# Attention on one core: value products of four key blocks in one run, row maxima of two score products by one VectorE instruction

## The chip, the cores and the metric

One core of one Trainium2 chip runs the whole program. The metric is the device time of one execution in microseconds (us); a run's time is that of this core. Smaller is better.

## The reference, cut to what matters

One decoder layer over 4096 tokens of width 1024: an RMSNorm, one input projection, three token mixers that share its columns, one output projection with a residual, and a final RMSNorm. The change touches only the third mixer, a causal attention with a cumulative forget bias, eight heads of width 64:

```python
for blk in range(seq // 128):
    s = einsum('bhqd,bhkd->bhqk', qh[blk], kh[:, :, :q1]) * scale
    s = s + c[:, :, q0:q1, None] - c[:, :, None, :q1]     # c: cumulative log forget gate
    s = where(mask, s, -inf)                              # causal inside the last block
    p = softmax(s, axis=-1)
    outs.append(einsum('bhqk,bhkd->bhqd', p, vh[:, :, :q1]))
```

Everything is float32.

## The kernel before, in words

Phase 1 (the first 1660 us of the profiled span) projects the tokens, runs the other two mixers and stores the attention's operands in DRAM. Phase 3 (the last 360 us) is the output projection. Phase 2 between them is the attention, and the change is there.

Phase 2 walks through 32 *units*: a pair of heads p (4 of them) by a group Q of 512 queries (8 of them), in the order p, then Q. A unit (p, Q) has 4(Q+1) *steps*, one for each block kb of 128 keys, 576 steps in all. The last four steps of a unit are its diagonal ones, where the number of live queries falls from 512 to 384, 256 and 128. Four steps that share one tile of 512 keys are called a *group* here; there are 144.

Two computations run side by side in the steps:

- The **second pass** (the loop `for si, (u, kb)`, whose products stand on lines 1353 and 1356). For each of two heads TensorE makes a score tile `st` [128 keys, 512 queries] in PSUM from two accumulating products (`ka` with `qa`, `kb` with `qc`). ScalarE writes `pt = exp(st + bias)` to SBUF (L1360). In diagonal steps GpSimd sets the masked corner of `pt` to zero (L1365). One step later `do_pv` adds two 64-column value products into the PSUM tile `pv` (L1238; the heads use the two halves of the array's columns; the operands are plain float32 where all score products are float32r) and adds `pt` into running sums `acc`, head 0 on VectorE and head 1 on GpSimd (both L1247).
- The **row-maximum pass** (the generator `rowmax`) works on later units. Each of its steps is one product `sm` [128 queries, 512 keys] (L128) into a PSUM bank, and one VectorE maximum along its rows into a column of `mp` (L137; where the last key tile is diagonal, a masked maximum, L132). The main loop advances it twice in each step, once before and once after `do_pv`, and a third time while it is less than LEAD = 76 products ahead. At the end of a unit `rm_tail` combines the maxima (`mm`, `m2`) and, some products later, transposes them on TensorE (`mt`, L1166); VectorE copies them out (`mr`, L1168).

When a unit's last value product is issued, `finish_unit` starts, one stage in each later step: two products of `ones_v` with the sums (`pl`, L1206), then on ScalarE a logarithm and an exponential of it (L1210, L1211), on VectorE `rt<-pl` (L1213) and L1214, on GpSimd two products (L1215, L1216), on VectorE `rt<-pv` (L1218), and the store.

PSUM has eight banks: two buffers of `st`, two of `pv`, and four one-bank buffers of the pool `ps_sm`, which `sm`, `mt`, `pl` and phase 3's `o` take in turn. `pt` has seven buffers. TensorE's order is as the program writes it (`manual_schedule`); the order of the other engines' instructions is chosen by the tile framework's scheduler, and each engine then executes its list in order.

## Time and profile before

| | |
|---|---|
| three runs | 3496.33, 3509.1 and 3524.09 us (median 3509.1) |
| span of the profiled execution (no separate time of it is listed) | 3516.6 us |
| mean granted TensorE clock | 0.982 |
| phase 2, 1660 to 3158 us: TensorE busy | 1469.9 of 1498 us |
| the same stretch: VectorE / ScalarE / GpSimd busy | 1251.7 / 737.3 / 897.9 us |

How to read it: TensorE has two rows, PE for the products and PEld for the loading of weights, which goes on beside the products. Matmul rows carry a modelled end, so the cost of a product is read from the start of one to the start of the next rather than from its own duration. A row "x4" of `pv` is the two heads' products of one key block: each is executed as two, and the two heads' run at the same time.

### The profile page before, as it was taken

The page shows a single profiled execution, that of the slowest core. Times are in us where ns is not written, and L with a number is a line of the kernel's source. Part 1 is how long each engine was busy: PE and PEld are TensorE (multiplying, and loading weights), DVE is VectorE, ACT ScalarE, POOL GpSimd, SP SyncE. Part 2 cuts the span into 40 slices and gives each one's busy share as a digit, 9 for nine tenths or more (in the row PEclk, how much of TensorE's full clock was granted, in tenths as well). Part 3 has the DMA queues.
Part 4 walks back from the last instruction along what each step waited for, and adds up shares of the span by engine and source line. Part 5 has one row for each costly group of instructions (what it writes and reads, how often), then busy time and mean ns, then how long its engine had stood idle before and what let it go on. Part 6 is the DMA issues. An engine that isn't in the chain of part 4 may idle for free.

```text
span 3516.6 us, 63564 instructions
## 1 busy us (share of the span) xinstructions
PE 3417.2 (97%) x24375; PEld 2569.8 (73%) x24375; DVE 2482.6 (71%) x5111; ACT 1584.4 (45%) x2883; POOL 1422.0 (40%) x1468
## 2 busy tenths in 40 slices
PE   7999999999999999988999999999999999999999
PEld 7999999999999998988444444444444444448887
DVE  6467746685467756782798878888889888965554
ACT  6335544356435543452345445454544554562221
POOL 2134422333134322352465466555665666570000
PEclk9999999999999999999799899999999999999999
DMA  5332333214332223212731141014101321013442
GB/s 178 109 94 64 97 127 116 79 53 159 97 104 68 70 85 111 67 49 78 155 77 34 49 118 43 19 41 120 55 28 28 97 64 37 28 64 135 148 146 96
DMA packets 227603, 297.75 MB, mean 85 GB/s; under 512 B 19602, under 2 KB 172448, under 8 KB 227298
## 3 DMA queue, kind: packets, MB, share of 16 engines
q1 hardware_dynamic: 227298, 293.69, 27.7%
q8 instruction: 191, 3.13, 0.4%
q14 instruction: 114, 0.93, 0.1%
HBM read 208.96 MB, written 84.43 MB: 83 GB/s over the span
## 4 chain that ended last, share of the span: by engine, by line
PE 76%; DVE 13%; ACT 4%; POOL 3%; issue 2%; DMA 2%; SPq 0%; DVEq 0%; POOLq 0%; ACTq 0%
PE acc L885 15%; PE pv L1238 13%; PE acc L906 12%; PE o L1430 10%; PE sm L128 9%; PE st L1353 7%; PE st L1356 6%; DVE wlo L211 2%; DVE acc L1247 1%; DMA x<-in_x_dram 1%; DVE mp L137 1%; PE pl L1206 1%; DVE gt L729 1%; DVE xq L494 1%; PE plb L557 1%
## 5 line engine op out<-in xcount | busy, mean ns | idle before, releaser
L1360 ACT ACTIVATE pt<-st,bias 128x512 f32<-128x512 f32 (+3 forms) x1152 | 692.0, 648 | 711.3 <-PE st L1356 699.3
L1247 POOL TENSOR_TENSOR acc<-acc,pt 128x512 f32<-128x512 f32 (+3 forms) x544 | 700.4, 1288 | 479.9 <-ACT pt L1360 469.4
L137 DVE TENSOR_REDUCE mp<-sm 128x1 f32<-128x512 f32 x896 | 590.1, 682 | 100.1 <-PE sm L128 92.3
L1238 PE MATMUL pv<-pt,v 128*64 128x512 f32 (+3 forms) x2304 | 587.7, 589 | 7.2 <-POOL pt L1365 4.5
L885 PE MATMUL acc<-hhi,whi 128*128 128x256 f32 x2048 | 580.7, 288 | 4.2 <-DVE q L718 2.3
L885 PE MATMUL acc<-hhi,wlo 128*128 128x256 f32 x2048 | 568.1, 282 | 0.0
L885 PE MATMUL acc<-hlo,whi 128*128 128x256 f32 x2048 | 567.3, 281 | 0.0
L906 PE MATMUL acc<-whi,hhi 128*128 128x256 f32 (+1 forms) x1792 | 518.3, 289 | 18.6 <-DVE gu L727 16.0
L1247 DVE TENSOR_TENSOR acc<-acc,pt 128x512 f32<-128x512 f32 (+3 forms) x544 | 506.5, 931 | 40.9 <-ACT pt L1360 30.4
L128 PEld LDWEIGHTS sm<-kb,qb 66*128 66x128 f32 x1152 | 218.1, 192 | 416.6 <-DVE mp L137 177.4
L906 PE MATMUL acc<-wlo,hhi 128*128 128x256 f32 (+1 forms) x1792 | 507.3, 283 | 0.0
L906 PE MATMUL acc<-whi,hlo 128*128 128x256 f32 (+1 forms) x1792 | 506.9, 283 | 0.0
L128 PE MATMUL sm<-kb,qb 66*128 66x512 f32 (+2 forms) x1152 | 494.2, 436 | 5.9 <-DVE mp L137 4.5
L1353 PE MATMUL st<-qa,ka 128*128 128x512 f32 (+2 forms) x1152 | 449.3, 392 | 12.4 <-DMA ka<-d_kl 12.4
L1356 PE MATMUL st<-qc,kb 68*128 68x512 f32 (+2 forms) x1152 | 442.3, 386 | 1.1 <-DMA qc<-d_m 1.1
L885 PEld LDWEIGHTS acc<-hhi,whi 128*128 128x128 f32 x2048 | 385.0, 190 | 7.8 <-DVE q L718 2.7
L885 PEld LDWEIGHTS acc<-hlo,whi 128*128 128x128 f32 x2048 | 384.2, 190 | 0.3 <-DVE hlo L273 0.2
L885 PEld LDWEIGHTS acc<-hhi,wlo 128*128 128x128 f32 x2048 | 384.3, 190 | 0.0
L906 PEld LDWEIGHTS acc<-whi,hhi 128*128 128x128 f32 x1792 | 341.9, 191 | 22.4 <-DVE gu L727 16.6
L906 PEld LDWEIGHTS acc<-wlo,hhi 128*128 128x128 f32 x1792 | 342.3, 191 | 0.1
L906 PEld LDWEIGHTS acc<-whi,hlo 128*128 128x128 f32 x1792 | 341.7, 191 | 0.0
L211 DVE SCALAR_TENSOR_TENSOR wlo<-wraw,gT,whi 128x256 fp32r<-128x256 f32 (+1 forms) x480 | 268.6, 600 | 58.1 <-ACT whi L210 56.8
(262 smaller groups left out, 4911.1 us busy)
## 6 DMA issues: line engine op xcount, KB each, us to landing
wraw<-in_w_in_dram SPq DMA_DIRECT2D x120, 512.0 KB
x<-in_x_dram SPq DMA_DIRECT2D x88, 512.0 KB
qa<-d_qh SPq DMA_DIRECT2D x64, 256.0 KB
out_dram<-x SPq DMA_DIRECT2D x31, 512.0 KB
kb<-d_kh SPq DMA_DIRECT2D x38, 256.0 KB
d_kh<-chi SPq DMA_DIRECT2D x32, 256.0 KB
d_kl<-clo SPq DMA_DIRECT2D x32, 256.0 KB
d_qh<-chi SPq DMA_DIRECT2D x32, 256.0 KB
```

Source lines behind the costliest of these rows:

```text
L128: nc.tensor.matmul(ps[:, :n], qb[0:66, h, i * P : (i + 1) * P], kb[0:66, h, :n], start=True, stop=True)
L137: nc.vector.tensor_reduce(dst, ps[:, :use], axis=AX.X, op=ALU.max)
L211: nc.vector.scalar_tensor_tensor(lo[:, k, :n], raw, g, hi[:, k, :n].bitcast(F32), op0=ALU.mult, op1=ALU.subtract)
L494: nc.vector.tensor_tensor(xq[rows, :, r, :].rearrange("p g (n h) -> p g n h", h=h), sl(e), sl(qf), op=ALU.mult,)
L885: nc.tensor.matmul(ps[:, a, :], ww[:, k, cs], hh[:, k, :], start=n == 0, stop=n == 3 * KC - 1)
L906: nc.tensor.matmul(o, hh[:, k, ts_], ww[:, k, :width], start=n == 0, stop=n == 3 * KC - 1)
L1238: nc.tensor.matmul(pv[64 * h : 64 * h + 64, q0:], vt[:, kb % 4, 64 * h : 64 * h + 64], pts[h][:, q0:], start=kb == 0, stop=kb == nkb - 1,)
L1247: eng.tensor_tensor(a[:, q0:], a[:, q0:], pts[h][:, q0:], op=ALU.add)
L1353: nc.tensor.matmul(st[:, qm:], ka_t[g][:, h, cs], qa_t[u % 2][:, h, qm:], start=True, stop=False)
L1356: nc.tensor.matmul(st[:, qm:], kb_t[g][0:68, h, cs], qc_t[u % 2][:, h, qm:], start=False, stop=True)
L1360: nc.scalar.activation(pt[:, q0:], st[:, q0:], AF.Exp, bias=bias_of[u][:, h, kb : kb + 1])
L1430: nc.tensor.matmul(ps, a[:, k % 4, o : o + P], b[k][:, cs], start=n == 0, stop=n == 3 * KC - 1)
```

## The change

It has four parts.

1. **Value products by groups.** `do_pv(u, j, group)` is called once for four steps, in the first step of the next group, after that step's scores and row-maximum products. It issues the eight value products of the group one after another. `pt` gets 13 buffers instead of 7.
2. **Sums.** VectorE's four additions of a group are written behind those products, in the same call. GpSimd's addition is written right behind the exponentials of its own step.
3. **Row maxima in pairs.** `rm_pair` makes two `sm` products into the two banks of one tile and takes their maxima by one `tensor_reduce` of 2 x 512 elements (diagonal tiles still get one masked maximum each). A step of the loop advances the pass once, by a pair, and a second time while it is less than LEAD products ahead. The tail's transpose waits three pairs instead of six products.
4. **PSUM.** `ps_sm` has two buffers of two banks instead of four of one; `pl`, `mt` and `o` take turns with the pairs in these two.

```diff
-        ps_sm = p2.enter_context(tc.tile_pool(name="ps_sm", bufs=4, space=PSUM))
+        ps_sm = p2.enter_context(tc.tile_pool(name="ps_sm", bufs=2, space=PSUM))
-        pp = p2.enter_context(tc.tile_pool(name="pp", bufs=7))
+        pp = p2.enter_context(tc.tile_pool(name="pp", bufs=13))
...
+    def rm_pair(ps, qb, kb, hi_, diag, tri, mp, cj):
+        for n in range(2):
+            rm_matmul(ps[:, n, :], qb, kb, hi_ + n, diag)
+        if diag:
+            for n in range(2):
+                rm_max(ps[:, n, :], hi_ + n, True, tri, mp[:, hi_ + n, cj : cj + 1])
+        else:
+            rm_max(ps, hi_, False, tri, mp[:, hi_ : hi_ + 2, cj])
...
-                    for hi_ in range(8):
-                        ps = ps_sm.tile([P, 512], F32, tag="sm", name="sm")
-                        rm_product(
-                            ps, qb, kb_t[p * NJ + cj], hi_, cj == Q, tri, mp[:, hi_, cj : cj + 1]
-                        )
+                    for hi_ in range(0, 8, 2):
+                        ps = ps_sm.tile([P, 2, 512], F32, tag="sm", name="sm")
+                        rm_pair(ps, qb, kb_t[p * NJ + cj], hi_, cj == Q, tri, mp, cj)
...
+        def do_pv(u, j, group):
...
+            for kb, pts in group:
+                q0, _ = q0_of(u, kb)
+                for h in (1, 0):
+                    nc.tensor.matmul(
+                        pv[64 * h : 64 * h + 64, q0:], vt[:, kb % 4, 64 * h : 64 * h + 64], pts[h][:, q0:],
+                        start=kb == 0, stop=kb == nkb - 1,
+                    )
+            for kb, pts in group:
+                do_acc(u, kb, 0, pts[0])
...
+            group.append((kb, pts))
             rm_step()
-            if pend is not None:
-                do_pv(*pend)
-            pend = (u, kb, pts)
-            rm_step()
+            do_acc(u, kb, 1, pts[1])
             if rm_count[0] < 2 * si + LEAD:
                 rm_step()
+            if kb % 4 == 0 and pend is not None:
+                do_pv(*pend)
+                pend = None
+            if kb % 4 == 3:
+                pend, group = (u, kb // 4, group), []
             tick(fin)
```

Other lines move the release of key and value slots into `do_pv`, and drop comments. Phase 1 and phase 3 are the same but for the pool that phase 3's `o` comes from.

TensorE in the middle of a unit, before: `st` are the scores of a step, `sm` row-maximum products, `pv` the value products of the step ahead.

```order
L1238 MATMUL pv<-pt,v 64x512 x2
L128 MATMUL sm<-kb,qb_21728 128x512
L1353 MATMUL st<-qa_21724,ka 128x512
L1356 MATMUL st<-qc_21729,kb 128x512
L1353 MATMUL st<-qa_21724,ka 128x512
L1356 MATMUL st<-qc_21729,kb 128x512
L128 MATMUL sm<-kb,qb_21728 128x512
L1238 MATMUL pv<-pt,v 64x512 x2
L128 MATMUL sm<-kb,qb_21728 128x512
```

The same place with the change:

```order
L1377 MATMUL st<-qc_21730,kb 128x512
L127 MATMUL sm<-kb,qb_21726 128x512 x2
L1374 MATMUL st<-qa_21725,ka 128x512
L1377 MATMUL st<-qc_21730,kb 128x512
L1374 MATMUL st<-qa_21725,ka 128x512
L1377 MATMUL st<-qc_21730,kb 128x512
L127 MATMUL sm<-kb,qb_21726 128x512 x2
L1265 MATMUL pv<-pt,v 64x512 x8
L1374 MATMUL st<-qa_21725,ka 128x512
L1377 MATMUL st<-qc_21730,kb 128x512
L1374 MATMUL st<-qa_21725,ka 128x512
L1377 MATMUL st<-qc_21730,kb 128x512
```

Value products stood alone between row-maximum products in every step; now eight follow each other, and then four steps have none.

TensorE where one unit ends and the next begins, with the change:

```order
L1181 MATMUL mt<-ident,m_31034 16x128
L127 MATMUL sm<-kb,qb_21727 128x512 x2
L1265 MATMUL pv<-pt,v 64x512 x2
L1265 MATMUL pv<-pt,v 64x384 x2
L1265 MATMUL pv<-pt,v 64x256 x2
L1265 MATMUL pv<-pt,v 64x128 x2
L1374 MATMUL st<-qa_21725,ka 128x512
L1377 MATMUL st<-qc_21730,kb 128x512
L1374 MATMUL st<-qa_21725,ka 128x512
L1377 MATMUL st<-qc_21730,kb 128x512
L127 MATMUL sm<-kb,qb_21727 128x512 x2
L1221 MATMUL pl<-acc_30998,ones_v 64x512
```

`mt` and `pl` each take one of the two `ps_sm` buffers between two pairs; `pl` comes in the second step of the new unit.

VectorE at such a boundary, before (`rt<-pl` is the step of `finish_unit` that frees the buffer of `pl`):

```order
L1247 TENSOR_TENSOR acc_29118<-acc_29118,pt 128x512
L137 TENSOR_REDUCE mp<-sm 128x1 x2
L1247 TENSOR_TENSOR acc_29118<-acc_29118,pt 128x512
L137 TENSOR_REDUCE mp<-sm 128x1
L1213 TENSOR_TENSOR rt<-pl,rc 128x512
L137 TENSOR_REDUCE mp<-sm 128x1
L1214 TENSOR_SCALAR rt<-rt 128x512
L137 TENSOR_REDUCE mp<-sm 128x1
```

and with the change:

```order
L1252 TENSOR_TENSOR acc_28510<-acc_28510,pt 128x512
L140 TENSOR_REDUCE mp<-sm 128x2
L1252 TENSOR_TENSOR acc_28510<-acc_28510,pt 128x512
L140 TENSOR_REDUCE mp<-sm 128x2
L1228 TENSOR_TENSOR rt<-pl,rc 128x512
L140 TENSOR_REDUCE mp<-sm 128x2
L1229 TENSOR_SCALAR rt<-rt 128x512
L140 TENSOR_REDUCE mp<-sm 128x2
L1252 TENSOR_TENSOR acc_28510<-acc_28510,pt 128x512
L1233 TENSOR_TENSOR rt<-pv,rc 128x512
L1252 TENSOR_TENSOR acc_28510<-acc_28510,pt 128x512 x2
L140 TENSOR_REDUCE mp<-sm 128x2 x3
```

One maximum stands where two stood. The sums, written together behind the value products, do not stay together: the scheduler puts the sums of the first steps ahead of those steps' maxima and the others between later ones.

## The prediction

> **What bounds the kernel now.** I read the page's busy times first, then the busy times by stretch of time, then the timeline of single steps.

> ```profile
> PE 3417.2 (97%) x24375; PEld 2569.8 (73%) x24375; DVE 2482.6 (71%) x5111; ACT 1584.4 (45%) x2883; POOL 1422.0 (40%) x1468
> ```
> ```profile
> 1660.00:3158.00 1498.00, 1469.85 (x5880) 717.08 (x5879) 1251.73 (x2163) 737.33 (x1226) 897.85 (x930) 0.98 0.24 63
> 2200.00:2500.00 300.00, 297.64 (x1219) 146.47 (x1216) 255.49 (x464) 147.92 (x250) 183.16 (x194) 1.00 0.23 62
> ```

> The columns of the second fence are the stretch, its length, then TensorE's products, its weight loads, VectorE, ScalarE and GpSimd. In attention TensorE is busy 1470 of 1498 us, VectorE 84%, ScalarE 49%. Over 2200 to 2500 us TensorE pauses for 2.4 us in 300: no wait is left to remove, only TensorE's own time. How that is spent shows in one step:

> ```profile
> 2202.30 0.20 PEld L1238 LDWEIGHTS pv<-pt,v 128*64 128x64 f32 x4 [0.36 <-issue]
> 2202.30 1.08 PE L1238 MATMUL pv<-pt,v 128*64 128x512 f32 x4
> 2203.31 0.50 PE L128 MATMUL sm<-kb,qb 66*128 66x512 f32 x1
> 2203.65 0.40 PE L1353 MATMUL st<-qa,ka 128*128 128x512 f32 x1
> 2203.89 0.40 PE L1356 MATMUL st<-qc,kb 68*128 68x512 f32 x1
> 2204.13 0.40 PE L1353 MATMUL st<-qa,ka 128*128 128x512 f32 x1
> 2204.33 1.27 ACT L1360 ACTIVATE pt<-st,bias 128x512 f32<-128x512 f32 x2 [1.35 <-PE st L1356]
> 2204.36 0.39 PE L1356 MATMUL st<-qc,kb 68*128 68x512 f32 x1
> 2204.59 0.39 PE L128 MATMUL sm<-kb,qb 66*128 66x512 f32 x1
> 2204.91 1.08 PE L1238 MATMUL pv<-pt,v 128*64 128x512 f32 x4
> ```

> Read starts. Score and row-maximum products follow each other every 0.235 us. The one after the value products holds its place for 0.34 (3.31 to 3.65), the one ahead of them for 0.32 (4.59 to 4.91), the value products of a block for 1.01. A step is 2.61 us.

> **Part 1, value products in runs.** What does a second block cost right behind the first? Near the end one `pv` is followed by products of the same shape, `pl`:

> ```profile
> 3089.21 1.08 PE L1238 MATMUL pv<-pt,v 128*64 128x512 f32 x4
> 3090.12 1.03 PE L1206 MATMUL pl<-acc,ones_v 128*64 128x512 f32 x4
> 3091.08 0.50 PE L1353 MATMUL st<-qa,ka 128*128 128x512 f32 x1
> ```

> Both take 1.87 us (3089.21 to 3091.08), so the second costs 1.87 - 1.01 = 0.86. Alone, a block costs 1.01 + 0.34 + 0.32 = 1.67 with its two neighbours; in a run 0.86 + 2 x 0.235 = 1.33. Each block that gets a neighbour ahead of it saves 0.34 us: three in each of 144 groups, 432 x 0.34 = **147 us**. A run of four costs 3.59, and with the longer products around it 3.78.

> Does the next block's weight load hide there?

> ```profile
> L1238 PEld LDWEIGHTS pv<-pt,v 128*64 128x64 f32 x2304 | 115.0, 136 | 202.3 <-issue 176.9 <-POOL pt L1365 10.4 <-POOL acc L1247 10.4
> ```

> A load takes 0.136 us; the four of a block are done 0.20 us after 2202.30, under products that run to 2203.38, and the 0.86 above leaves no room for one in the open. [...]

> **What shows behind the bound: ScalarE and two score buffers.** TensorE alone would need 24 x 0.235 + 3.78 = 9.42 us for four full steps, against 4 x 2.61 = 10.45. But four steps now come without value products between them, 6 x 0.235 = 1.41 us each, and a score buffer is not back that fast. A place near the end where a score product waits for its buffer:

> ```profile
> 3133.46 1.26 ACT L1360 ACTIVATE pt<-st,bias 128x512 f32<-128x512 f32 x2
> 3134.19 0.19 PEld L1353 LDWEIGHTS st<-qa,ka 128*128 128x128 f32 x1 [0.86 <-ACT pt L1360]
> 3134.53 0.40 PE L1356 MATMUL st<-qc,kb 68*128 68x512 f32 x1
> 3134.77 0.19 PEld L1353 LDWEIGHTS st<-qa,ka 128*128 128x128 f32 x1 [0.28 <-ACT pt L1360]
> 3134.97 1.32 ACT L1360 ACTIVATE pt<-st,bias 128x512 f32<-128x512 f32 x2 [0.25 <-PE st L1356]
> ```

> The exponentials end at 3134.72, the load starts 0.05 later, the second product 0.34 after the first load (4.19 to 4.53), the exponential 0.44 after that (4.97), and one takes 0.68: 0.05 + 0.34 + 0.44 + 0.68 = 1.51 us round a buffer. The load that waits cannot hide, which is 0.11 of it. From the end of a run (t = 0): scores at 0 and 0.47; exponentials 0.67 to 1.35 and, 0.59 behind, 1.26 to 1.94; the next scores at 1.51 and 2.10, then 3.03 and 3.61, then 4.54 and 5.13; the run at 6.06 instead of 5.64. So 0.42 lost, and a stretch of four full steps takes 9.84. There are 84 stretches with nothing else in them: **+35**. Bounds: 0.12 each if the load hides (+10), 0.42 (+35); I take the row's.

> **Parts 2 and 3, VectorE.** The new maximum over 2 x 512 is in no row. From below, by the slope of the masked maxima; from above, twice the old one:

> ```profile
> L137 DVE TENSOR_REDUCE mp<-sm 128x1 f32<-128x512 f32 x896 | 590.1, 682 | 100.1 <-PE sm L128 92.3
> L132 DVE CUSTOM_DVE_ANT_0 sm<-sm,tri 128x512 f32<-128x512 f32 x64 | 44.5, 695 | 4.0 <-PE sm L128 3.7
> L132 DVE CUSTOM_DVE_ANT_0 sm<-sm,tri 128x256 f32<-128x256 f32 x64 | 27.6, 431 | 6.9 <-PE sm L128 6.9
> L1247 DVE TENSOR_TENSOR acc<-acc,pt 128x512 f32<-128x512 f32 x448 | 457.0, 1020 | 33.7 <-ACT pt L1360 30.4 <-POOL pt L1365 1.8
> L1247 POOL TENSOR_TENSOR acc<-acc,pt 128x512 f32<-128x512 f32 x448 | 623.4, 1392 | 474.4 <-ACT pt L1360 469.4
> L1365 POOL TENSOR_SCALAR_AFFINE_SELECT pt<-pt 128x128 f32<-128x128 f32 x256 | 83.9, 335 | 69.1 <-ACT pt L1360 66.2
> ```

> (695 - 431) / 256 = 1.03 ns an element, so 682 + 528 = 1210 ns; twice 682 is 1364. I take 1.21, since no second start is paid. Instructions in a row start some 0.09 before the last one ends, so 1.13 a maximum. A sum takes 0.69 undisturbed, 0.60 to the next start:

> ```profile
> 2202.43 0.69 DVE L1247 TENSOR_TENSOR acc<-acc,pt 128x512 f32<-128x512 f32 x1
> 2203.04 1.50 DVE L137 TENSOR_REDUCE mp<-sm 128x1 f32<-128x512 f32 x2
> ```

> Four of each: 4 x (1.13 + 0.60) = 6.9 us of 9.84. VectorE was not the bound and is not now, so its saving is worth nothing by itself: the work that hides it is TensorE's 9.42. In a full stretch the fourth pair (4.1) wants the buffer of the second-last maximum (done 3.2): no wait. Were the maximum 1.36, still none.

> **Part 4, two buffers: the boundaries.** `pl` holds one of two buffers until `rt<-pl`. Before, with four:

> ```profile
> 2230.05 1.08 PE L1206 MATMUL pl<-acc,ones_v 128*64 128x512 f32 x4
> 2231.18 0.60 ACT L1210 ACTIVATE rc<-pl 128x512 f32<-128x512 f32 x1 [1.89 <-PE pl L1206]
> 2231.84 1.27 ACT L1360 ACTIVATE pt<-st,bias 128x512 f32<-128x512 f32 x2
> 2232.99 0.63 ACT L1211 ACTIVATE rc<-rc 128x512 f32<-128x512 f32 x1
> 2234.60 0.68 DVE L1213 TENSOR_TENSOR rt<-pl,rc 128x512 f32<-128x512 f32 x1
> ```

> It was held 5.2 us (2230.05 to 2235.28). Now, in a unit's first full stretch, `pl` stands at 1.50 and takes 1.20 of TensorE. The logarithm comes 1.13 later (2.63), scores of the next step at 2.61, exponentials 3.28 to 4.55, ScalarE's second instruction to 5.08. VectorE's order puts a sum (to 4.6) and a maximum (to 5.73) ahead of `rt<-pl`, which ends at 6.42. The pair of the step after wants that buffer at 5.17 and starts 6.42 + 0.05 + 0.11 = 6.58: 1.41 lost, about 1.6 with ScalarE's share. 28 units: **+46**. Queued behind the waiting pair are the next scores, the run and all that feeds on them. Bounds: 0.9 if the sum comes behind `rt<-pl`, 3 if both additions meet GpSimd's.

> In diagonal steps the scores are shorter:

> ```profile
> 2219.49 0.18 PE st L1353
> 2221.87 0.12 PE st L1353
> ```

> Steps are then 1.18, 0.95 and 0.95 us on TensorE, less than a maximum (1.13) behind a sum that waits for GpSimd's 0.34. The third pair waits 0.3 for its buffer and scores wait 0.5 for ScalarE: 0.8 x 32 = **+26**. `mt` uses up a buffer's turn (29 times, always ahead of a run), so the pair behind it needs the maximum just started: about 0.6 each, **+17**. Three units of one group get `pl` in a diagonal stretch: 1.5 each, **+5**. Last, when the row maxima have run out:

> ```profile
> 3109.45 1.08 PE L1238 MATMUL pv<-pt,v 128*64 128x512 f32 x4
> 3111.60 0.65 PE L1238 MATMUL pv<-pt,v 128*64 128x512 f32 x2
> ```

> 2.15 a step, 8.6 a group. With the run, two score buffers at 1.51 give 5.59 + 3.78 = 9.37: each of 8 groups loses 0.77 instead of saving 1.02 - 0.42 = 0.60, together **+11**.

> The opening (three products a step before, two pairs now, until 76 ahead) I leave at 0, between -10 and +10.

> Sum: -147 + 35 + 46 + 26 + 17 + 5 + 11 = **-7 us**, 3509.6 against the span of 3516.6. That execution lies 7.5 us over the median of the runs, so on the runs' scale 3509.1 - 7 = **3502**. About 1%, 35 us, is what a measurement of this kernel tells from no change. Nearly all that the runs save goes back to waits that two score buffers and two `ps_sm` buffers open.

> **Rivals.**

> - *The waits are mostly hidden.* Late loads cost 0.12 instead of 0.42 in a stretch (-25), boundaries half (-23 and -13). 3502 - 61 = 3441. For: VectorE has 3 us of slack in a stretch. Against: the 1.51 us round trip is read off rows. 0.28.
> - *Slower: `pl` keeps its buffer longer.* The additions' rows say 1020 and 1392 ns on average where an undisturbed VectorE one takes 0.69: VectorE and GpSimd disturb each other, and in the new order sums and `rt<-pl` fall where GpSimd adds. If a boundary costs 2 us more than forecast, 31 x 2 = 62: 3564. It decides from (35 + 7) / 31 = 1.4 us more. Against: in the run VectorE catches up. 0.16. [...]
> - *Loads show in the run.* If each further block's load stood in the open, 3 x 0.136 x 144 = 59 us would come on top: 3561. The `pl` rows and the four loads done in 0.20 us speak against it: 0.04. [...]
> - *The change does not do what it says* in one point already: the order shows the sums scattered, not together. Were they executed in the run, boundaries would lose the 0.6 of the sum ahead of `rt<-pl`, 28 x 0.6 = 17 us less; that is inside the forecast's range. Something else that gains over 1%, the opening for one: 0.02.

> **How the numbers follow.** Forecast 0.50, rivals 0.28, 0.16, 0.04 and 0.02. Within 1% is the forecast, 0.50; faster 0.28 + 0.02 = 0.30; slower 0.16 + 0.04 = 0.20. The range holds 8 in 10: down to the first rival's 3441, up to 3550, short of the slower ones' 3561 and 3564. The forecast's own range is 3475 to 3540.

> **What would show it.** Right: the second to fourth blocks of a run 0.86 apart; score loads waiting for `pt` in the steps between runs, with about 9.8 us from run to run; the pair after `pl` waiting over 1 us for `rt`; the new maximum near 1.2 us; TensorE's busy share in attention down from 98% to about 90%. Wrong: a run to run of 9.4, no wait behind `pl`, or blocks in a run 1.0 apart.

## The result, and the profile after

The kernel before took 3512.2 us (median of 6 runs), the changed one 3541.4 (6 runs): ratio 1.0085, 95% interval 1.0065 to 1.0106. That is 29 us slower, clear of the noise, where 7 us faster was forecast. The profiled executions have spans of 3516.6 and 3539.7 us.

The page's busy times of the changed kernel:

```profile
PE 3390.0 (96%) x24375; PEld 2603.3 (74%) x24375; DVE 2377.4 (67%) x4675; ACT 1606.0 (45%) x2883; POOL 1399.5 (40%) x1468
```

TensorE is busy 27 us less and VectorE 105. By stretches of time, with the columns as in the prediction and the granted clock behind GpSimd's count:

```profile
1660.00:3182.00 1522.00, 1444.37 (x5895) 751.81 (x5893) 1146.48 (x1727) 759.32 (x1226) 875.32 (x930) 0.97 0.23 62
2066.50:3177.00 1110.50, 1065.08 (x4354) 548.23 (x4352) 841.45 (x1256) 571.57 (x922) 657.45 (x693) 0.98 0.18 53
```

The second row is the part of attention that belongs to the last three pairs of heads (p = 1 to 3). The same units in the kernel before:

```profile
2073.00:3153.10 1080.10, 1071.44 (x4353) 519.67 (x4352) 912.33 (x1567) 555.01 (x922) 673.80 (x690) 1.00 0.19 54
```

They take 1110.5 instead of 1080.1 us, 30.4 more, and the clock over them is no longer full: the records of the granted clock list nine windows of 3.4 or 6.8 us at half clock there, 54.6 us together, and none before. The first pair of heads is 8.5 us shorter (390.8 against 399.3), the rest of the span 1.2 longer: 30.4 - 8.5 + 1.2 = 23.1.

**The runs and the score buffers are as forecast.** A full stretch, from a run to the next:

```profile
2247.25 3.65 PE L1265 MATMUL pv<-pt,v 128*64 128x512 f32 x16
2250.83 0.50 PE L1374 MATMUL st<-qa,ka 128*128 128x512 f32 x1
2252.34 0.19 PEld L1374 LDWEIGHTS st<-qa,ka 128*128 128x128 f32 x1 [0.28 <-ACT pt L1381]
2252.34 0.50 PE L1374 MATMUL st<-qa,ka 128*128 128x512 f32 x1
2253.85 0.50 PE L1374 MATMUL st<-qa,ka 128*128 128x512 f32 x1
2255.49 0.40 PE L1374 MATMUL st<-qa,ka 128*128 128x512 f32 x1
2257.20 3.65 PE L1265 MATMUL pv<-pt,v 128*64 128x512 f32 x16
```

Four blocks take 3.58 us (47.25 to 50.83), against 3.59 forecast. The next two steps are 1.51 us apart, with the score load waiting for ScalarE: the round trip of a score buffer. The third is 1.64. From run to run it is 9.95.

The same groups of instructions, by shape:

```profile
L140 DVE TENSOR_REDUCE mp<-sm 128x2 f32<-128x1024 f32 x436 | 524.2, 1219 | 26.2 <-PE sm L127 25.2
L1252 DVE TENSOR_TENSOR acc<-acc,pt 128x512 f32<-128x512 f32 x448 | 386.9, 864 | 203.3 <-ACT pt L1381 192.4 <-POOL pt L1386 2.6
L1252 POOL TENSOR_TENSOR acc<-acc,pt 128x512 f32<-128x512 f32 x448 | 608.4, 1358 | 491.6 <-ACT pt L1381 486.5
```

The new maximum is 1.22 us (forecast 1.21). The sums got faster on average, 0.86 instead of 1.02.

**The boundary waits are there, at other places than forecast.** In the first full stretch of a unit (p = 1, Q = 5) the pair of the third step behind the run waits:

```profile
2233.28 1.22 DVE L140 TENSOR_REDUCE mp<-sm 128x2 f32<-128x1024 f32 x1
2234.42 0.68 DVE L1228 TENSOR_TENSOR rt<-pl,rc 128x512 f32<-128x512 f32 x1
2234.56 0.73 PE L127 MATMUL sm<-kb,qb 66*128 66x512 f32 x2 [0.54 <-DVE mp L140]
2241.18 0.69 DVE L1233 TENSOR_TENSOR rt<-pv,rc 128x512 f32<-128x512 f32 x1 [2.39 <-POOL rc L1231]
2241.79 2.44 DVE L1252 TENSOR_TENSOR acc<-acc,pt 128x512 f32<-128x512 f32 x2
2244.15 3.47 DVE L140 TENSOR_REDUCE mp<-sm 128x2 f32<-128x1024 f32 x3
2245.41 0.73 PE L127 MATMUL sm<-kb,qb 66*128 66x512 f32 x2 [0.80 <-DVE mp L140]
```

The first wait (0.54) is for a maximum, not for `rt<-pl`: the pair starts at 2234.56, while `rt<-pl` still reads `pl` until 2235.10, so it does not use `pl`'s buffer. It waits for the maximum of the pair just ahead of it (2233.28 to 2234.50), so it takes that pair's buffer, while `pl` holds the other; experiment e4 bears this out. The second (0.80) comes a stretch later, where none was forecast: VectorE waits 2.39 us for GpSimd at `rt<-pv`, then two sums take 2.44 where undisturbed they would take 1.3, and the maxima are late. The step with the first wait is 2.44 us long and the one with the second 2.64, instead of 1.57.

**Then the clock halves.** In these traces the granted clock changes only on a grid of 3.413 us: all 44 of its records after the change, and all 28 before, begin a whole number of times 3.413 us from the first, to within 0.01. The time from one point of the grid to the next is called a *slot* here, and one or more slots at half clock a *window*. Five neighbouring slots in a small unit (p = 2, Q = 2):

```profile
2486.07:2489.49 3.42, 3.42 (x17) 1.59 (x13) 2.24 (x5) 1.26 (x2) 2.95 (x2) 1.00 0.00 0
2489.49:2492.90 3.41, 2.42 (x10) 1.38 (x10) 3.38 (x9) 2.71 (x4) 2.85 (x3) 1.00 0.46 154
2492.90:2496.31 3.41, 3.41 (x8) 2.25 (x8) 3.41 (x9) 1.36 (x2) 1.75 (x2) 0.50 0.25 76
2496.31:2499.73 3.42, 3.42 (x9) 1.01 (x10) 2.68 (x8) 0.01 (x1) 1.55 (x2) 0.50 0.00 1
2499.73:2503.14 3.41, 3.41 (x18) 1.71 (x14) 0.00 (x0) 0.91 (x2) 0.26 (x1) 1.00 0.00 0
```

In the second slot TensorE has waits, the longest 0.99 us. The next two run at half clock, and the rows there show it:

```profile
2492.79 1.05 PE L127 MATMUL sm<-kb,qb 66*128 66x384 f32 x2 [0.99 <-DVE mp L135]
2493.63 0.63 PE L1374 MATMUL st<-qa,ka 128*128 128x512 f32 x1
2494.06 0.63 PE L1377 MATMUL st<-qc,kb 68*128 68x512 f32 x1
2494.49 0.63 PE L1374 MATMUL st<-qa,ka 128*128 128x512 f32 x1
```

Score products start 0.43 us apart instead of 0.235. With that, half of the windows' length is counted as lost, an estimate: 27.3 of 54.6 us for p = 1 to 3. In all of attention (with the first pair of heads, which lost 28.1 before and 21.2 now) the half clock costs 20.4 us more than before. Without it the change would have come out at 23.1 - 20.4 = +3 us, against the forecast -7.

All the runs say the same, not only the profiled ones, since each has its span and its mean granted clock on record, and span x (1 - clock) is what the half clock takes by the same estimate. The kernel before loses 57 us in the mean of 63 runs, the changed one 84 in its six; what remains of the span is 3455 and 3457 us. So the changed order costs next to nothing at full clock, and 28 of the 29 us are the clock's. From run to run of one kernel the remainder scatters by 1 to 4 us (standard deviation), the loss by up to 11.

### The profile page after: what moved, and what is told of

Same layout as the page of the kernel before. It is cut to its first block, busy times and chain, and to the rows that moved or that the text cites. A ratio compares the mean times of both kernels' runs of the same rounds, so it can differ in the third digit from the quotient of the medians.

```text
span 3539.7 us, 63110 instructions
## 1 busy us (share of the span) xinstructions
PE 3390.0 (96%) x24375; PEld 2603.3 (74%) x24375; DVE 2377.4 (67%) x4675; ACT 1606.0 (45%) x2883; POOL 1399.5 (40%) x1468
## 4 chain that ended last, share of the span: by engine, by line
PE 69%; DVE 16%; ACT 5%; POOL 4%; issue 3%; DMA 2%; SPq 0%; DVEq 0%; POOLq 0%; ACTq 0%
PE acc L902 15%; PE pv L1265 11%; PE acc L923 11%; PE o L1455 10%; PE st L1374 7%; PE sm L127 6%; PE st L1377 5%; DVE mp L140 3%; DVE wlo L228 2%; DVE acc L1252 2%; ACT pt L1381 2%; DMA x<-in_x_dram 1%; POOL acc L1252 1%; POOL rc L1231 1%; PE pl L1221 1%
## 5 line engine op out<-in xcount | busy, mean ns | idle before, releaser
L1381 ACT ACTIVATE pt<-st,bias 128x512 f32<-128x512 f32 (+3 forms) x1152 | 716.6, 650 | 749.3 <-PE st L1377 731.7
L1252 POOL TENSOR_TENSOR acc<-acc,pt 128x512 f32<-128x512 f32 (+3 forms) x544 | 680.4, 1251 | 497.1 <-ACT pt L1381 486.5
L1252 DVE TENSOR_TENSOR acc<-acc,pt 128x512 f32<-128x512 f32 (+3 forms) x544 | 429.7, 790 | 266.1 <-ACT pt L1381 192.4
L140 DVE TENSOR_REDUCE mp<-sm 128x2 f32<-128x1024 f32 (+1 forms) x460 | 539.8, 1192 | 53.8 <-PE sm L127 52.8
L1374 PE MATMUL st<-qa,ka 128*128 128x512 f32 (+2 forms) x1152 | 511.9, 445 | 21.8 <-DMA v<-d_v 12.7
L1265 PE MATMUL pv<-pt,v 128*64 128x512 f32 (+3 forms) x2304 | 508.3, 585 | 0.8 <-POOL pt L1386 0.8
L1374 PEld LDWEIGHTS st<-qa,ka 128*128 128x128 f32 x1152 | 218.8, 190 | 313.0 <-ACT pt L1381 180.0
L127 PE MATMUL sm<-kb,qb 66*128 66x512 f32 (+2 forms) x1152 | 365.7, 401 | 51.5 <-DVE mp L140 38.2
L1265 PEld LDWEIGHTS pv<-pt,v 128*64 128x64 f32 x2304 | 158.8, 142 | 294.0 <-issue 267.4
```

Source lines behind the costliest of these rows:

```text
L127: nc.tensor.matmul(ps[:, :n], qb[0:66, h, i * P : (i + 1) * P], kb[0:66, h, :n], start=True, stop=True)
L140: nc.vector.tensor_reduce(dst, ps, axis=AX.X, op=ALU.max)
L1252: eng.tensor_tensor(a[:, q0:], a[:, q0:], pt[:, q0:], op=ALU.add)
L1265: nc.tensor.matmul(pv[64 * h : 64 * h + 64, q0:], vt[:, kb % 4, 64 * h : 64 * h + 64], pts[h][:, q0:], start=kb == 0, stop=kb == nkb - 1,)
L1374: nc.tensor.matmul(st[:, qm:], ka_t[g][:, h, cs], qa_t[u % 2][:, h, qm:], start=True, stop=False)
L1381: nc.scalar.activation(pt[:, q0:], st[:, q0:], AF.Exp, bias=bias_of[u][:, h, kb : kb + 1])
```

## Experiments

In each table row: time and ratio to the kernel before; then, from the profiled execution, the time of the units p = 1 to 3, what of it is lost at half clock (half the length of its windows), and the difference, which is what the instructions' order costs at full clock. The kernel before was run again beside each set and took 3509.9 to 3514.5 us; the ratios are to those runs. The table's right half is one execution of each kernel, some 13 us over its kernel's median for e2 and 13 under for e10. p = 0 is left out: its time lies between 373 and 410 us, of which 4 to 43 are lost at half clock; without them it is 365 to 376.

| kernel | us | ratio, 95% interval | p = 1 to 3 | lost | rest |
|---|---|---|---|---|---|
| before | 3512.2 | | 1080 | 0 | 1080 |
| changed | 3541.4 | 1.0085 (1.0065 to 1.0106) | 1110 | 27 | 1083 |
| e1 runs only | 3590.4 | 1.023 (1.0193 to 1.0266) | 1156 | 60 | 1096 |
| e2 pairs only | 3536.0 | 1.0071 (1.0049 to 1.0094) | 1104 | 20 | 1084 |
| e3 runs, 3 + 3 buffers | 3609.7 | 1.0279 (1.025 to 1.0308) | 1160 | 101 | 1060 |
| e4 `pl` copied | 3615.1 | 1.0295 (1.0265 to 1.0324) | 1170 | 70 | 1100 |
| e5 pairs, runs, alternate | 3563.2 | 1.0135 (1.0098 to 1.0172) | 1123 | 36 | 1087 |
| e6 runs, alternate | 3555.4 | 1.012 (1.0093 to 1.0147) | 1126 | 38 | 1088 |
| e8 filler | 3541.3 | 1.008 (1.0051 to 1.011) | 1105 | 12 | 1093 |
| e9 changed, fewer GpSimd adds | 3504.7 | 0.9975 (0.996 to 0.999) | 1080 | 15 | 1065 |
| e10 before, fewer GpSimd adds | 3495.8 | 0.995 (0.9928 to 0.9971) | 1072 | 0 | 1072 |
| e11 runs of two | 3499.2 | 0.9954 (0.9936 to 0.9971) | 1081 | 10 | 1071 |
| e12 pairs, runs of two | 3499.1 | 0.9969 (0.995 to 0.9988) | 1078 | 7 | 1071 |
| e13 runs of two, 3 + 3 buffers | 3506.3 | 0.9977 (0.9963 to 0.9991) | 1085 | 20 | 1065 |

### The parts alone: e1, e2

e1, against the changed kernel:

```diff
-        ps_sm = p2.enter_context(tc.tile_pool(name="ps_sm", bufs=2, space=PSUM))
+        ps_sm = p2.enter_context(tc.tile_pool(name="ps_sm", bufs=4, space=PSUM))
-                    for hi_ in range(0, 8, 2):
-                        ps = ps_sm.tile([P, 2, 512], F32, tag="sm", name="sm")
-                        rm_pair(ps, qb, kb_t[p * NJ + cj], hi_, cj == Q, tri, mp, cj)
+                    for hi_ in range(8):
+                        ps = ps_sm.tile([P, 512], F32, tag="sm", name="sm")
+                        rm_product(
+                            ps, qb, kb_t[p * NJ + cj], hi_, cj == Q, tri, mp[:, hi_, cj : cj + 1]
+                        )
...
             rm_step()
+            rm_step()
```

e2 is the reverse: the kernel before with `rm_pair`, two two-bank buffers and one `rm_step` fewer a step.

> Part 1 alone: value products still issued in runs of four blocks, but row maxima one product at a time as before, with four one-bank ps_sm buffers. Theory (the runs save what was forecast, 1.02 us a group, and two ps_sm buffers with the row maxima in pairs give it back at the unit boundaries and, through the half-clock windows that follow those waits, in the small units): a full stretch takes about 9.8 to 9.95 us as in the changed kernel (two score buffers are unchanged), the first stretch of a unit about the same instead of 11.65, no half-clock windows between 2000 and 3150 us; 84 x -0.5, 28 x -0.6, 32 x -0.6, +11 at the end: about -75, so 3435 (3415 to 3460). Rival (the runs themselves cost what they save, through VectorE's four sums in a row or the loads): 3510 to 3550 in this kernel too.

> Parts 2 to 4 alone: row maxima in pairs with two two-bank ps_sm buffers, value products and sums after every step as before. Theory: a pair comes only every 2.61 us instead of every 1.51, so the buffer that pl holds for 5 us is wanted 5.2 us later and the wait is short; 0 to 25 us slower than before (3512 to 3537), and few half-clock windows. Rival (two buffers cost their 60 to 70 us whatever the spacing of the steps): 3560 to 3580.

e1 went against my theory: the runs alone, with all four buffers, are slower than the whole change. Its timeline in the second stretch of a unit:

```profile
2246.75 5.96 DVE L1254 TENSOR_TENSOR acc<-acc,pt 128x512 f32<-128x512 f32 x4
2249.11 1.38 POOL L1254 TENSOR_TENSOR acc<-acc,pt 128x512 f32<-128x512 f32 x1 [0.30 <-ACT pt L1383]
2250.69 1.47 POOL L1254 TENSOR_TENSOR acc<-acc,pt 128x512 f32<-128x512 f32 x1 [0.20 <-ACT pt L1383]
2252.63 3.67 DVE L140 TENSOR_REDUCE mp<-sm 128x1 f32<-128x512 f32 x6
2253.36 1.39 PE L127 MATMUL sm<-kb,qb 66*128 66x512 f32 x2 [3.60 <-DVE mp L140]
```

Four sums in a row hold VectorE for 5.96 us, 5.64 of them in the sums themselves, because GpSimd is adding most of the time; no maximum comes in between, and TensorE waits 3.60 us. (Not all are like this: the 32 rows of four between 1990 and 3100 us take 5.49 in the mean, 3.71 in sums and the rest in waits.) Over p = 1 to 3 there are 19 waits for such a maximum, 40 us together, and 19 windows at half clock, one of them from 2252.7 on for 6.8 us. That GpSimd is the cause shows in VectorE's smallest instructions in the same place of another unit, on tiles of 8 columns:

```profile
2193.45 2.85 POOL L1254 TENSOR_TENSOR acc<-acc,pt 128x512 f32<-128x512 f32 x2 [1.22 <-ACT pt L1383]
2193.64 1.26 DVE L163 TENSOR_TENSOR mm<-mm,cref 128x8 f32<-128x8 f32 x1
2194.93 0.17 DVE L169 TENSOR_SCALAR m<-mm 128x8 fp32r<-128x8 f32 x1
2195.14 1.17 DVE L170 SCALAR_TENSOR_TENSOR m<-mm,m 128x8 fp32r<-128x8 f32 x1
```

The two that read two SBUF tiles take 1.26 and 1.17 us, the second of them to 2196.31, where GpSimd's row ends at 2196.30; the one that reads one takes 0.17. In the changed kernel the first of them (L163) takes 0.158 in the median and 1.204 at most:

```profile
L163 DVE TENSOR_TENSOR mm<-mm,cref x28: 148/158/1204, 1352.0 to 3086.4; 128x8 f32<-128x8 f32 x28
```

The longest of them, from 2338.47 to 2339.67, stands beside an addition of GpSimd from 2338.38 to 2339.65. So in these rows VectorE's instruction on 8 columns with two SBUF inputs ended with the addition of GpSimd that it met.

In e2 the theory held for the order (1084, 4 us over before) and missed the clock: five windows of together 41 us. Its time is at the upper end of the range.

### Buffers: e3, e4

e3 is e1 with `ps_st` and `ps_sm` at three one-bank buffers each. In e4 ScalarE copies `pl` first:

```diff
+            nc.scalar.copy(t, pl)
-            nc.scalar.activation(r, pl, AF.Ln)
+            nc.scalar.activation(r, t, AF.Ln)
...
-            nc.vector.tensor_tensor(t, pl, r, op=ALU.mult)
+            nc.vector.tensor_tensor(t, t, r, op=ALU.mult)
```

> Runs of four blocks, row maxima one product at a time, three score buffers and three one-bank ps_sm buffers. Theory (the 0.42 us a stretch is the round trip of two score buffers): scores no longer wait in the steps between runs, pitch 1.41 to 1.45 instead of 1.51 to 1.62, a full stretch 9.45 to 9.6; 0.4 x 144 below the kernel with runs and four ps_sm buffers, about 3385 to 3410 if three ps_sm buffers are enough at the boundaries. Rival (ScalarE itself, 2 x 0.68 a step with the logarithms between, sets 1.5): stretch 9.9 as before, 3430 to 3460.

> The changed kernel, but ScalarE copies pl to SBUF first, so that its ps_sm buffer comes free about 0.6 us after pl and waits for no VectorE instruction; the correction then reads the copy. Theory (the boundary wait is pl's hold on one of two buffers, and the half-clock windows follow from it): the pair's wait for rt<-pl is gone (28 x -1.2), 31 copies of 0.6 cost ScalarE up to 19, and half-clock windows in units of one to three groups get fewer (up to -20): about 3505 (3490 to 3520). Rival (VectorE's backlog sets the boundary, pl's buffer only shows it): the wait moves to the next pair's maximum and the time stays within 10 of the changed kernel's 3541.

e3: the third score buffer does bring time, the rest is 1060, 37 us under e1's; a full stretch from a unit's fourth group on takes 9.66 us in the median against 9.97 (9.45 to 9.6 was expected). But TensorE can run only three maxima ahead; it waits up to 4.3 us for one, and 24 windows at half clock take 101 us:

```profile
2270.13 4.85 DVE L1254 TENSOR_TENSOR acc<-acc,pt 128x512 f32<-128x512 f32 x4
2275.63 0.80 PE L127 MATMUL sm<-kb,qb 66*128 66x512 f32 x1 [4.29 <-DVE mp L140]
```

e4 is 74 us slower than the changed kernel, where 36 us of gain were expected. The correction now reads two SBUF tiles and, like the sums, takes longer beside GpSimd's additions (1.73 us); the scheduler then put two sums ahead of the next maximum:

```profile
2255.27 1.73 DVE L1229 TENSOR_TENSOR rt<-rt,rc 128x512 f32<-128x512 f32 x1
2262.38 3.06 DVE L1253 TENSOR_TENSOR acc<-acc,pt 128x512 f32<-128x512 f32 x2
2266.63 1.22 PE L127 MATMUL sm<-kb,qb 66*128 66x512 f32 x2 [2.43 <-DVE mp L140]
```

With `pl` in PSUM that instruction took 0.68. The theory was right on the wait that it named. The pair of the first stretch no longer waits, and its step takes 1.67 us in nearly every unit instead of 2.44:

```profile
2251.84 0.63 PE L127 MATMUL sm<-kb,qb 66*128 66x512 f32 x2
2253.47 0.62 PE L127 MATMUL sm<-kb,qb 66*128 66x512 f32 x2
```

So that wait is `pl`'s hold on one of two buffers. But the copy made the second stretch worse: the step with its wait takes 4.0 to 4.7 us in most units instead of 2.64, and the time lies above theory and rival. From this a new theory was formed: sums in a row meet GpSimd, and the waits halve the clock.

### The place of the sums: e5, e6

VectorE's sums are issued one a step, a step late, and queued behind a maximum, the next maximum behind the sum; e5 on the changed kernel, e6 on e1.

```diff
             do_acc(u, kb, 1, pts[1])
+            if prev is not None:
+                do_acc(*prev)
+            prev = (u, kb, 0, pts[0])
...
-            for kb, pts in group:
-                do_acc(u, kb, 0, pts[0])
```

> The changed kernel, but VectorE's sums are issued one a step (a step late) and queued alternately with the maxima, instead of up to three in a row; value products still in runs of four, maxima in pairs, two ps_sm buffers. Theory (formed after the first four experiments: three or four sums in a row meet GpSimd's additions and take 4 to 5.5 us, for which no maximum comes and TensorE's row-max products wait for a buffer): the wait in the second stretch of a unit goes (28 x 1.0 to 1.2), and with it some half-clock windows: 3505 (3485 to 3520). Rival (two buffers and pl alone set the wait; the sums' place does not matter): 3535 to 3550.

> Value products in runs, row maxima one product at a time, four one-bank ps_sm buffers (as in the run with part 1 alone), but one sum queued after every two maxima. Theory (that run lost its gain to four sums in a row, 5.5 us with GpSimd adding beside them, and to the half clock after the waits): the waits of 1.9 to 3.6 us for a maximum and nearly all half-clock windows between 2000 and 3150 us go, a full stretch stays at 9.9, and the time is 3435 to 3465, faster than before. Rival (the runs themselves cost it): above 3550 as with part 1 alone.

By the numbers both theories failed: e5 lies above its rival's range too, and e6 in its rival's. e6 takes 35 us off e1, 22 of them at half clock, and stays slower than before. e5 is slower than the changed kernel. One sum at a time still meets one addition of GpSimd (mean 1.01 us in e6), and four steps of 1.5 us, in which GpSimd hardly pauses (1.42 us for an addition, in the mean), stay what they were. The order of the sums sharpens the loss but does not make it.

### The cause apart: e9, e10

In both, GpSimd's additions of the second head are left out in all full steps, so its weight sums are incomplete. (e7, which left them out in the diagonal steps too, has no time.)

```diff
-            else:
+            elif h == 0 or diag:
                 eng.tensor_tensor(a[:, q0:], a[:, q0:], pt[:, q0:], op=ALU.add)
```

> The changed kernel with GpSimd's additions of the second head left out in all full steps (the first block's copy and the diagonal steps' additions are kept, so the second head's weight sums are incomplete). Theory (a VectorE instruction with two SBUF inputs waits for the addition that GpSimd is in, and in four steps of 1.5 us GpSimd adds nearly without a break): sums take 0.69 in full stretches, the 84 us of waits of row-max products for maxima fall to under 30, the half-clock windows behind them mostly go, and the time is about 3480 (3455 to 3505). Rival (the wait is for pl's buffer, or for the maxima themselves): 3525 to 3545.

> Control: the kernel before with the same additions of GpSimd left out. Theory (there GpSimd pauses 1.2 us in every step of 2.6, and VectorE has time): sums fall from 1.02 to 0.7 us but the time stays within 1%, 3495 to 3512. Rival (GpSimd's additions cost both kernels alike): 50 us or more come off here too.

By the ratios e9 is 1.1%, 39 us, faster than the changed kernel, at the upper end of what was expected, and e10 19 us faster than before, as its theory had it. So 20 us of e9's gain belong to the new order. In p = 1 to 3 it is 30 us for e9 and 8 for e10: 22, of which 12 are lost at half clock and 10 are not. The second stretch of the same unit as above (p = 1, Q = 5), in e9:

```profile
2224.43 0.69 DVE L1233 TENSOR_TENSOR rt<-pv,rc 128x512 f32<-128x512 f32 x1 [1.67 <-POOL rc L1231]
2225.04 2.27 DVE L1252 TENSOR_TENSOR acc<-acc,pt 128x512 f32<-128x512 f32 x3
2227.23 2.35 DVE L140 TENSOR_REDUCE mp<-sm 128x2 f32<-128x1024 f32 x2
2227.64 0.63 PE L127 MATMUL sm<-kb,qb 66*128 66x512 f32 x2
```

Three sums in the time of two, and the pair waits for nothing: the step is 1.57 us instead of 2.64. The step of the first stretch stays at 2.43. So the wait in the second stretch is GpSimd's, and the one in the first, which e4 showed to be `pl`'s, is not. TensorE's waits for a maximum, p = 1 to 3, in the changed kernel and in e9 (us in total, times, longest):

```profile
PE sm L127 <- DVE mp L140: 30.3, 49, 0.9
```
```profile
PE sm L127 <- DVE mp L140: 17.0, 35, 0.9
```

### The clock: e8

```diff
+                if diag and Q <= 2:
+                    nc.tensor.matmul(st, ka_t[g][:, h, cs], qa_t[u % 2][:, h, :], start=True, stop=True)
```

> The changed kernel with one more 512-column product ahead of each pair of score products in the diagonal steps of the units of one to three key groups, written over at once by the score product (96 products, 22 us of TensorE at full clock). Theory (the clock is set in slots of 3.413 us, and one in which TensorE's products fill less than about 0.55 is followed by half clock): these sparse slots fill up, the half-clock windows between 2000 and 3150 us (nine, 27 us lost) go or fall to three at most, and the time stays within 3525 to 3550 in spite of the added work. Rival (a single wait of about a microsecond causes them): they stay, and the time is 3555 to 3565.

The time did not change although TensorE does 96 products more. In p = 1 to 3 the windows fell from nine (27.3 us lost) to six, 23.9 us together (11.9 lost), where none to three were expected, and none is left in the units with Q = 1, where the changed kernel had three; Q = 2 went from 33.5, 36.6 and 33.6 us to 31.3, 31.8 and 32.8, with 1.9 us of products added to each. Other units got windows instead (Q = 4: 50.5 to 52.4 and 52.9). Adding work to a place with waits kept the clock up and paid for itself. In the units with Q = 2 the wait itself stays, 0.99 us each time: half clock follows it only where its slot is filled to 0.50, and not in the two filled to 0.55 and 0.57, while in the changed kernel (0.51 in all three) it followed each time. That speaks for the share of a slot as the cause, and against the single wait. In the units with Q = 0 and 1 the filler took the waits of 0.9 us away as well, so they do not tell the two apart.

All 14 profiled executions say the same. Cut into the slots of 3.413 us at which the records of the clock change, 2050 to 3150 us, with 0.235 us for each 512 columns: of 81 full-clock slots that TensorE filled to under 0.50, 79 were followed by half clock; of 143 between 0.50 and 0.65, 49; of 4033 over 0.65, one. (The counts move by a few with the way in which a product across a slot's edge is shared out.) The slot 2489.49 above was filled to 0.51. Most slots under 0.50 had a wait of over 1.1 us, but a shorter wait does not decide: of the slots whose longest wait was 0.6 to 1.1 us, half clock followed 34 of 77 that were filled to under 0.65, and none of 55 that were filled to more. In the changed kernel waits of 0.6 to 1.0 us were enough in slots that the products filled to 0.51 to 0.59.

### Shorter runs: e11, e12, e13

```diff
-            if kb % 4 == 0 and pend is not None:
+            if kb % 2 == 0 and pend is not None:
...
-            if kb % 4 == 3:
+            if kb % 2 == 1:
                 pend, group = (u, kb // 4, group), []
```

e11 has this on e1, e12 on the changed kernel, e13 is e11 with three score and three `ps_sm` buffers.

> Value products and sums of two blocks together instead of four, row maxima one product at a time, four one-bank ps_sm buffers. Every second block saves 0.34 us: 288 x 0.34 = 98; two score buffers cost about 0.1 a pair, 29. Theory (bursts of four steps are what VectorE, GpSimd and the clock do not bear; two steps and then 1.9 us of value products keep TensorE's share of each 3.4 us slot near one): no wait over 1 us in full stretches, few half-clock windows, 3445 (3430 to 3480), faster than before. Rival (any run costs more than it saves): 3515 to 3560.

> As the last, but with the changed kernel's maxima in pairs and two two-bank ps_sm buffers. Theory: the gain of the runs of two less the boundaries of two buffers, which cost 27 us by the run with pairs alone: 3475 (3455 to 3505). Rival (pairs win because VectorE has less to do): as fast as or faster than one product at a time, 3430 to 3450.

> The kernel with runs of two blocks and maxima one product at a time, with three score buffers and three one-bank ps_sm buffers instead of two and four. Theory (in runs of two the second step still takes 1.51 us for two score buffers, 5.09 to 5.10 a pair against 4.88 for TensorE alone; VectorE, with one or two sums in a row, gives three ps_sm buffers back in time): a pair of steps takes 4.9, 240 pairs x 0.2 = 48 less than with two score buffers, about 3455 (3440 to 3485). Rival (as with runs of four, the missing fourth ps_sm buffer lets TensorE wait for maxima, over 50 us of such waits between 2000 and 3150 us, and half-clock windows follow): 3500 to 3550.

e11 and e12 are faster than before, by 0.46% and 0.31%, so the rival of e11 is out; but the gain is 15 us, not 69. Two steps take 1.51 + 3.58 = 5.09 us where two took 2 x 2.62 = 5.24: 0.15 a pair, where 0.24 was forecast, and windows at half clock take 10 of it back. In e13 the third score buffer lowers the rest to 1065 again and the missing fourth `ps_sm` buffer takes it back: TensorE waits 38.4 us for maxima (14.8 in e11) and loses 20 at half clock. Its time is in the rival's range; the third score buffer is worth 6 us at full clock, where 48 was forecast.

No version that does all the work beats the kernel before by more than 0.5%.

## Why the prediction was wrong

- **Part 1, right.** A run 3.58 against 3.59; second to fourth blocks 0.86 apart; the loads do not show: inside the run two of 0.14 us start every 0.43, beside products that run on.
- **Score buffers, right.** 1.51 us round a buffer, 9.95 a stretch against 9.84 forecast; 84 x 0.11 = 9 us too little.
- **Parts 2 and 3, the maximum right (1.22), the sums mis-sized.** "A sum takes 0.69 undisturbed, 0.60 to the next start": I took the undisturbed value although the quoted row said 1020 ns on average. From it followed that in a full stretch the fourth pair has "no wait". In the second stretch of most units with Q of 2 and over the step is 2.64 - 1.57 = 1.07 longer, some 24 us in all that had no term. e9 takes just this wait away.
- **Part 4, the buffer right, the boundary over-sized.** `pl`'s hold on a buffer does set this wait (e4), and `rt<-pl` ends 6.53 us behind the run, 6.42 by the forecast. But the pair takes the other buffer, which a maximum frees earlier, and starts at 5.99 instead of 6.58. Forecast some 1.6 a unit; measured 2.44 - 1.57 = 0.87, and 0.53 in the units with Q of 4 and 7: some 22 us in all instead of 46. This error and the one before cancel by luck, as -7 forecast and +3 measured without the clock show.
- **`mt`, over-sized.** Forecast 0.6 for the pair behind it; in p = 1 to 3 these pairs wait 0 to 0.67 us, 0.35 in the mean: 29 x 0.25 = 7 us too much.
- **Diagonal steps, right:** the last three of a unit take 3.96 us in most units, against 1.18 + 0.95 + 0.95 + 0.8 = 3.88. The tail nearly: the last unit is 9.5 us longer (76.1 against 66.6), 1.7 of it lost at half clock; forecast were 8 x 0.77 = 6.2 for its groups, and at most some 2.4 for its boundary and its diagonal steps.
- **The step that failed is the sum itself:** it charges every wait with its own length. "TensorE's busy share in attention down from 98% to about 90%" stands in the prediction as a thing to look for, and it was not followed to what the clock does where that share falls. (Over all of attention it is 95%, 1444 of 1522 us.) The clock fell to half for nine windows in p = 1 to 3, eight of them in units of one to three groups, where a unit's waits fall close together: +20 us over all of attention in the profiled executions, and 28 of the 29 us by all runs: the whole difference between "no change" and what was measured.
- **Rivals.** "`pl` keeps its buffer longer" named the disturbance of VectorE by GpSimd, rightly, and put it at the wrong place. "The waits are mostly hidden" and "loads show" did not occur. The order was read as showing the sums scattered; executed, most stand alone or three together (48 times three in a row between 1990 and 3100 us; 4.04 us each in the mean, 2.33 of them in sums and the rest in waits, mostly for exponentials).

What stays open: what decides in a slot that TensorE fills to between 0.50 and 0.65. Whether a filler at all boundaries of e3 or e13 would keep the clock up, where the order at full clock is 15 to 20 us better than before, was not tried.

## What to carry to other kernels

Grouping work on the bound engine makes bursts for the others: look at what each of them does in the shorter steps, instruction by instruction, and take durations from rows with the same neighbours, not from the undisturbed ones (a sum here: 0.69 us undisturbed, 1.02 in the mean before). Price a wait of TensorE twice, its length and the slots at half clock behind it (here 28 of 29 us), above all where the products around it are sparse. Runs of two here took part of the gain, 15 us, without the burst.
